# Marking the operations that empty matmul banks as first to be scheduled

## The chip, the cores and the metric

The kernel runs on one core of a Trainium2 chip. The core has a matrix unit (TensorE, "PE" in the profile; its weight loads are "PEld"), VectorE ("DVE"), ScalarE ("ACT"), GpSimd ("POOL") and SyncE ("SP"), whose queue issues most of the DMAs. Each engine works through its own list of instructions in order; between engines they wait on semaphores. The time is that of one execution on the device, in microseconds; the median of several runs is compared.

## The reference

One layer of a streaming encoder, applied to a prompt of 2048 tokens and, with carried state, to 8 samples of 16 tokens. The width is 1024, everything is fp32.

```python
def trunk_layer(x, pos, C0, n0, m0, k_cache, v_cache, conv_prev, mchunk, ...):
    qm, km, vm, om, ip, fp, qa, ka, va = split_in(x @ w_in)      # 4*512 | 8 | 512 | 2*128
    ...
    hm, C1, n1, m1 = mlstm_chunkwise(qm, km, vm, logi, logf, C0, n0, m0, mchunk)
    og = jax.nn.sigmoid(om.astype(jnp.float32)).reshape(B, T, M_HEADS, M_HEAD_DIM)
    hm = (og * head_norm(hm, g_mlstm_norm)).reshape(B, T, M_WIDTH).astype(x.dtype)
    qa = rope(qa.reshape(B, T, A_Q_HEADS, A_HEAD_DIM), pos)
    ka = rope(ka.reshape(B, T, A_KV_HEADS, A_HEAD_DIM), pos)
    ...                                                          # ha: sliding-window attention
    mix = jnp.concatenate([hm, ha], axis=-1) @ w_out
    h = layer_norm(DEEPNORM_ALPHA * x + mix, ln1_g, ln1_b)
    f, conv_rows = conv_ffn(h, conv_prev, w_up, w_conv, b_conv, w_down)
    y = layer_norm(DEEPNORM_ALPHA * h + f, ln2_g, ln2_b)
    return y, (C1, n1, m1, k_rows, v_rows, conv_rows)

def conv_ffn(h, conv_prev, w_up, w_conv, b_conv, w_down):
    u = h @ w_up                                                 # 1024 -> 2 * 2816
    ext = jnp.concatenate([conv_prev.astype(u.dtype), u], axis=1)
    c = b_conv + sum(ext[:, j:j + T] * w_conv[j] for j in range(CONV_W))
    a, g = jnp.split(c, 2, axis=-1)
    return (jax.nn.silu(g) * a) @ w_down, ext[:, -(CONV_W - 1):]
```

Four large projections hold nearly all of the arithmetic: the in-projection (w_in), the output projection (w_out), the up-projection (w_up) and the down-projection (w_down). The mLSTM (a matrix memory with gates), the attention over a window of 128 tokens, the norms, the width-3 convolution and the gate lie between them.

## The kernel before

**How a product is made.** PE multiplies numbers of reduced precision, so each fp32 operand is split into a high part (a cast on ACT, L217) and a low part (a subtraction on DVE, L218; for tokens L564 and L565), and each product is three matmuls: high by high, high by low, low by high. Most projections are cut into blocks of 2 by 2, and these are multiplied in the form that needs seven block products and not eight, numbered by s in the code. The sums of weight blocks and of token blocks that this form needs are made on DVE or read back from DRAM.

**Banks.** Products accumulate in matmul banks (512 fp32 values for each of 128 partitions). The in-projection has three, A, B and C. Products 1 and 2 go to A; 6, 5 and 3 to B; 7 and 4 to C. A bank's sum is carried on from one product to the next where the form allows it; after product 1 ACT copies A to B. Everything that leaves a bank is a copy by ACT or a sum by DVE, and a product that wants the bank anew waits until this operation is done. The order of the products is such that a bank is often read just after the product that fills it and wanted again soon after.

**The stages.** The in-projection (`i_dense`, to about 650 us) runs over token blocks b, column blocks g and the products s. After each product `i_after` empties the bank: copies (L769), the sum `add` (L775), and for g = 2 also the rotary embedding of four DVE operations (`rope`, L866 to L869), for g = 3 the gate's tanh, then the stores to DRAM by the SP queue (`i_store`, L751 for one of them). The mLSTM and the attention of earlier token blocks are woven in between the products by `Chains`: their matmuls stand between those of the projection in PE's list, and their other operations (for instance the mLSTM's output at L1164 to L1179, the attention's softmax at L1319 to L1344, that of the samples at L1502 to L1517) run on the same DVE, ACT and POOL. The output projection (`o_block`, about 650 to 925 us, five token blocks) has plain products; its banks are emptied by one DVE operation each, L1610, which adds the bank to the residual. The first four blocks are normed as they come; the last block's norm (`o_late`, loads L1634, sums L1638 and L1639) runs inside the next stage. The up-projection (`f_ups`, about 915 to 1860 us) runs over 3 token blocks, 22 column pairs j and seven products s, on two sets of three banks. `f_after` copies or adds each bank into the half-rows `u` (L1851 to L1870), and after products 3 and 4 it goes on with the convolution (L1882, L1884), the gate and the store. `f_next` makes the weights of a product 6 products ahead in the first token block, 8 in the others. The down-projection (`f_downs`, to the end) uses eight banks; `S.copy` (L2046) and `add` (L2063 to L2068) empty them into the rows `yacc`, which are normed and stored.

**What sets the order.** PE's list is written by hand: it is the order in which the program states its matmuls (`manual_schedule`, in `run`). The lists of DVE, ACT and POOL and the SP queue are made by the scheduler of the tile framework. It takes operations as they become ready by its own reckoning, and where several are ready it goes by priority, which is the order in which the program states them. Inside `with tc.high_priority():` operations get a priority ahead of all that isn't so marked. Before the change no copy or sum of the projections is marked. In `run`'s in-projection loop, `with self.tc.issue_after(behind)` holds weight loads behind the first copy of a column block.

Of the kernel before, what the change touches and what calls it, by code (L numbers as in the profile page):

```python
# [11 lines left out]
ALU = mybir.AluOpType  # L12
# [16 lines left out]
ALPHA = 2.0 ** 0.25  # L29
# [175 lines left out]
class Prog:  # L205
# [380 lines left out]
    def i_dense(self):  # L586
        nc, a = self.nc, self.a
        nb = len(IBLOCKS)
        last = NG - 1

        self.next_raw()
        self.x_load(0, 2)
        for _ in range(3):
            self.next_raw()
        self.x_load(0, 4)
        self.single_raw = self.tp.tile([P, KD, P], F32, name="xsr", tag="pth", bufs=2)
        nc.sync.dma_start(self.single_raw, a["xs"])
        self.angles = {}
        self.rope_load(IBLOCKS[0][2], 2)
        self.rope_load(NPT, 1)  # L600
        self.next_split()
        self.x_steps(0, "b12")
        for _ in range(3):
            self.next_split()
        self.x_steps(0, 3)
        self.x_single(1, 2)
        self.x_load(0, 1)
        self.next_raw()
        self.x_load(0, 3)
        self.x_steps(0, 1)  # L610
        self.advance()
        self.x_steps(0, 2, "t3", 7, "t2", 6)
        self.x_single(4)
        self.x_steps(0, "t1", 5, "t4")
        self.sb, self.trans = {}, None

        passages = [{1: ["load"], 7: ["t3", 7], 6: ["t2", 6], 3: [3, "t4"], 4: ["b12", "t1"]},
                    {1: ["load"], 6: ["t3"], 7: [7, "t2"], 5: [6], 3: [3, "t4"], 4: ["b12", "t1"]}]
        sums = 0
        after = None  # L620
        for item in self.items:
            if after:

                after[0] -= 1
                if after[0] == 3:
                    self.logs_of(after[1] - 1)
                if after[0] < 0:
                    self.i_done = after[1]
                    after = None
            self.chains.hold = item[0] == "t" and item[1] > 0  # L630
            if item[0] == "t":
                _, b, ti, e = item
                if ("g", e, 3) not in self.wu:
                    self.advance()
                if b not in self.gates:
                    self.gates[b] = self.tp.tile([P, 5, 8], F32, name="gates", tag="gates", bufs=2)
                ps = self.bank([P, 512], "pg") if ti == 4 else self.ib[ti % 2 * 2]
                yield from self.i_direct(b, ti, e, ps)
                self.i_keys(b, ti, ps)
                if ti == 1:  # L640
                    if b + 1 < nb:
                        self.x_steps(b + 1, 1, 2)
                    else:
                        self.release(4)
                    after = [6, b + 1]
                elif ti == 3 and b or ti == 4:
                    self.release(4)
                    self.x_steps(b, 4)
                    if b:
                        self.x_steps(b, 5)  # L650
                self.advance()
                continue
            _, b, g, s = item
            if item not in self.wu:
                self.advance()
            yield from self.i_product(b, g, s)
            del self.wu[item]
            self.release(2)
            if self.trans and s != 4:
                self.i_transposes()  # L660
            behind = self.i_after(b, g, s)
            if (b, g, s) == (0, 0, 7):
                self.t_setup()
            if (g, s) == (1, 6):
                self.rope_load(IBLOCKS[b][0], 2)
            if g == last and b + 1 < nb:
                if s == 7:
                    self.rope_load(IBLOCKS[b + 1][2], 2)
                for x in passages[b > 0].get(s, ()):
                    if x == "load":  # L670
                        self.spare = True
                        self.x_load(b + 1, 1, 2, 3, 4)
                    else:
                        self.x_steps(b + 1, x)
            if g == last and b + 1 == nb and s in (7, 5, 2, 3):
                self.x_pair(0, (7, 5, 2, 3).index(s))
            with self.tc.issue_after(behind) if behind and b == 0 else nullcontext():
                self.advance()

            if b >= nb // 2 and g < last:  # L680

                steps = (6, 2, 5) if g == last - 1 else (6, 5, 3)
                if s in steps:
                    self.d_sums(sums, steps.index(s))
                    sums += s == steps[2]
        self.sums = sums
        self.logs_of(nb - 1)
        self.chains.hold = False
# [897 lines left out]
    def o_block(self, b):  # L1586
        nc, nb = self.nc, len(OBLOCKS)
        tiles = OBLOCKS[b]

        ys = self.ynext + [self.o_x(t) for t in tiles[len(self.ynext):]]  # L1590
        self.ynext = []

        outs = [self.fp.tile([P, D], F32, name="ymix", tag="hst", bufs=2) for _ in tiles] if b == nb - 1 else ys
        for hf in range(2):
            c = slice(hf * 512, hf * 512 + 512)
            steps = 0
            for cost, ti, ps in self.group(b, tiles, 8 * b + 4 * hf, hf == 1):
                yield cost
                if ps is None:
                    steps += 1  # L1600
                    if hf and b + 1 < nb and steps == 8 * len(tiles) - 6:
                        self.ynext = [self.o_x(t) for t in OBLOCKS[b + 1][:2]]
                    if steps % 2 == 0 and self.norms and next(self.norms[0], self) is self:
                        del self.norms[0]
                    if hf == 0 and b and self.sums < NK2 and steps in (2, 14, 20):
                        self.d_sums(self.sums, (2, 14, 20).index(steps))
                        self.sums += steps == 20
                    continue
                y = outs[ti]
                nc.vector.scalar_tensor_tensor(y[:, c], ys[ti][:, c], ALPHA, ps, op0=ALU.mult, op1=ALU.add)  # L1610
                if hf and b < nb - 1:
                    self.norms.append(self.norm(y, *self.ln1, self.zh[tiles[ti]]))
        assert b < nb - 1 or self.sums == NK2
        self.late = list(zip(outs, tiles))
# [164 lines left out]
    def f_ups(self, n):  # L1779
# [11 lines left out]
        for i, (b, j, s) in enumerate(self.seq):  # L1791
# [4 lines left out]
            self.f_product(b, j, s)  # L1796
            while self.made < min(i + 1 + (AHEAD if b == 0 else AHEAD + 2), len(self.seq)):
                self.f_next()
            self.f_after(b, j, s)
            if i < 4:  # L1800
                self.f_tokens(0, *((5,), (3,), ("t4",), (4,))[i])
# [31 lines left out]
            for i, (l, r) in enumerate(((wh, hh), (wh, hl), (wl, hh))):  # L1833
                mm(ps, l[:, k], r[:, k], start=s in (1, 7) and k == 0 and i == 0, stop=k == 3 and i == 2, skip_group_check=True)  # L1834

    def f_after(self, b, j, s):

        nc, f2 = self.nc, self.f2
        V, S = nc.vector, nc.scalar
# [6 lines left out]
        dec = lambda z: z[:, m:].rearrange("p (b l) -> p b l", b=DB)  # L1846
        sam = lambda u: u[:, 2 + WP:2 + n].rearrange("p (b l) -> p b l", b=DB)
        m = WP - h
        half = lambda v: f2.tile([P, 770], F32, name=f"u{v}", tag=f"u{v}", bufs=1)
        if s == 1:  # L1850
            S.copy(B, A)  # L1851
        elif s == 6:
            self.u2[j % 2] = u2 = f2.tile([P, 384], F32, name="ua", tag="ua", bufs=2)[:, :h]
            S.copy(u2, B)
        elif s == 2:
            self.uv = half(0)
            S.copy(self.uv[:, 2:2 + h], A)
        elif s == 5:
            self.ug = u = half(1)
            u4 = f2.tile([P, 384], F32, name="ub", tag="ub", bufs=1)[:, :h]  # L1860
            S.copy(u4, B)
            V.tensor_add(u[:, 2 + h:2 + WP], C[:, :m], u4[:, :m])
            if has_s:
                V.tensor_add(sam(u)[:, :, 2:], dec(C), dec(u4))  # L1864
        elif s == 3:
            S.copy(self.uv[:, 2 + h:2 + WP], B[:, :m])
            if has_s:
                S.copy(sam(self.uv)[:, :, 2:], dec(B))
        elif s == 4:
            V.tensor_add(self.ug[:, 2:2 + h], C, self.u2[j % 2])  # L1870
        if s not in (3, 4):
            return

        v, u = (0, self.uv) if s == 3 else (1, self.ug)
        if v == 0:
# [130 lines left out]
    def f_downs(self):  # L2006
# [35 lines left out]
        def after(s, p):  # L2042
            ps = banks[role[s][2 if p == np_ else p]]
            ta, tb = (tiles[2 * np_], None) if p == np_ else (tiles[p], tiles[np_ + p])
            if s == 1:
                S.copy(banks[role[6][2 if p == np_ else p]], ps)  # L2046
            elif s == 2:
                add(ta, 0, ps, True)
                if ta == last_tile:
# [12 lines left out]

        def add(t, half, ps, first):  # L2063
            y = ys[t][:, half * 512:half * 512 + 512]
            if first:
                V.scalar_tensor_tensor(y, y, ALPHA, ps, op0=ALU.mult, op1=ALU.add)
            else:
                V.tensor_add(y, y, ps)  # L2068

        def finish(t, b, step):  # L2070
            if b == nb - 1 and step == 3:
# [68 lines left out]
```

## Time and profile before

| | |
|---|---|
| time, median of 3 runs | 2336.47 us (2332.86 to 2341.85) |
| profiled execution, its own time | 2337.74 us |
| its span | 2336.0 us |
| mean granted clock of PE | 0.992 |
| PE busy | 2300.5 us (98%) |
| DVE busy | 1818.7 us (78%) |
| ACT busy | 1275.2 us (55%) |
| POOL busy | 253.0 us (11%) |
| DMA | 629.24 MB, mean 269 GB/s |

The profile is that of one execution; the time runs from start to end on the device, the span from the first to the last instruction. Busy times count the work of an engine, not its waiting. The shares are averages over four stages: DVE, at 78% of the whole, is close to full in some stretches of tens of microseconds and has room in others. Rows name an operation by its engine, its line in the kernel and what it writes and reads (`zev<-dps,zev`: tile zev from a bank of the pool dps and zev). A wait is put down to the operation that came last.

### The profile page before, as it was taken

What the parts mean: (1) busy time and instruction counts of PE and PEld (TensorE: products, weight loads), DVE (VectorE), ACT (ScalarE), POOL (GpSimd) and SP (SyncE); (2) the same over time, 40 slices, a digit from 0 to 9 for tenths busy, and PEclk for the clock granted to TensorE, in tenths of its full rate; (3) what the DMA queues carried; (4) which work ended last, traced back from release to release, by engine and by line L of the source; (5) the groups of instructions that cost most, each with busy time, mean ns of one, the idle gap of its engine ahead of it and who ended that gap; (6) DMA issues with size and microseconds to landing.
All of it is one profiled execution on the core that took longest, in us unless ns stands there. A gap on an engine that the chain in (4) does not pass through costs nothing. (4 is left out here: it accounts for less than half of the span.)

```text
span 2336.0 us, 39880 instructions
## 1 busy us (share of the span) xinstructions
PE 2300.5 (98%) x14301; PEld 2112.0 (90%) x14301; DVE 1818.7 (78%) x3187; ACT 1275.2 (55%) x2409; POOL 253.0 (11%) x477
## 2 busy tenths in 40 slices
PE   8999999999999999999999999999999999999998
PEld 8999989998987777999999999999999978888876
DVE  7786587797688888988788776778766786896987
ACT  5453457776766664556556555556554544444452
POOL 0001000000011111211102010102111200100100
PEclk9999999999999999999999999999999999999999
DMA  7888889989987766788777889878998786756753
GB/s 271 293 304 294 285 271 337 318 291 330 327 274 251 233 214 250 268 319 295 265 275 267 311 310 318 304 266 279 308 299 262 224 288 197 258 175 226 251 157 108
DMA packets 298727, 629.24 MB, mean 269 GB/s; under 512 B 47709, under 2 KB 140961, under 8 KB 298529
## 3 DMA queue, kind: packets, MB, share of 16 engines
q1 hardware_dynamic: 294144, 612.99, 76.7%
q0 software_dynamic: 3520, 10.56, 1.4%
q10 hardware_dynamic: 864, 3.15, 0.3%
q8 instruction: 113, 1.85, 0.3%
q14 instruction: 86, 0.70, 0.1%
HBM read 456.01 MB, written 170.59 MB: 268 GB/s over the span
## 5 line engine op out<-in xcount | busy, mean ns | idle before, releaser
L1834 PE MATMUL fup<-hh,uw 128*128 128x384 f32 (+1 forms) x1848 | 480.7, 329 | 2.5 <-DVE uw L218 2.1
L1834 PE MATMUL dps<-hh,uw 128*128 128x384 f32 (+1 forms) x1848 | 478.7, 328 | 3.4 <-DVE u L1864 2.4
L1834 PEld LDWEIGHTS fup<-hh,uw 128*128 128x128 f32 x1848 | 331.6, 189 | 3.7 <-DVE uw L218 2.4
L1834 PEld LDWEIGHTS dps<-hh,uw 128*128 128x128 f32 x1848 | 330.2, 188 | 4.2 <-DVE u L1864 2.7
L1884 DVE SCALAR_TENSOR_TENSOR cc<-u,cw,cc 128x768 f32<-128x768 f32 (+1 forms) x264 | 258.4, 979 | 63.8 <-ACT cc L1882 57.6
L1834 PE MATMUL fup<-hl,uw 128*128 128x384 f32 (+1 forms) x924 | 303.7, 329 | 2.6 <-DVE hl L218 2.5
L1834 PE MATMUL dps<-hl,uw 128*128 128x384 f32 (+1 forms) x924 | 302.5, 327 | 0.0
L702 PE MATMUL dps<-w,oh 128*128 128x256 f32 x1344 | 257.2, 286 | 1.3 <-DVE zev L775 0.8
L217 ACT CAST uw<-wraw 128x1024 fp32r<-128x1024 f32 x126 | 123.0, 979 | 225.5 <-PE dps L2039 119.9
L218 DVE TENSOR_TENSOR w<-wraw,w 128x1024 fp32r<-128x1024 f32 (+2 forms) x167 | 189.0, 1139 | 55.4 <-ACT w L217 54.3
L217 ACT CAST w<-wraw 128x1024 fp32r<-128x1024 f32 (+2 forms) x167 | 162.9, 983 | 119.1 <-PE dps L702 57.1
L702 PEld LDWEIGHTS dps<-w,oh 128*128 128x128 f32 x1344 | 212.5, 189 | 12.8 <-issue 8.9
L218 DVE TENSOR_TENSOR uw<-wraw,uw 128x1024 fp32r<-128x1024 f32 x126 | 142.3, 1131 | 66.2 <-ACT uw L217 66.0
L702 PE MATMUL dps<-w,ol 128*128 128x256 f32 x672 | 188.8, 281 | 0.0
L1834 PEld LDWEIGHTS fup<-hl,uw 128*128 128x128 f32 x924 | 174.5, 189 | 3.3 <-DVE hl L218 3.2
L2039 PE MATMUL fup<-uw,fu 128*128 128x512 f32 x726 | 174.5, 396 | 1.7 <-DVE uw L218 1.7
L702 PE MATMUL dps<-oh,w 128*128 128x256 f32 x896 | 170.7, 285 | 5.3 <-ACT zev L769 3.2
L1834 PEld LDWEIGHTS dps<-hl,uw 128*128 128x128 f32 x924 | 173.6, 188 | 0.0
L2039 PEld LDWEIGHTS fup<-uw,fu 128*128 128x128 f32 x726 | 136.8, 189 | 35.2 <-DVE uw L218 2.1
L2039 PE MATMUL dps<-uw,fu 128*128 128x512 f32 x660 | 165.2, 395 | 1.1 <-DVE uw L218 1.1
L1882 ACT ACTIVATE cc<-u,cw 128x768 f32<-128x768 f32 (+1 forms) x132 | 132.2, 1002 | 56.4 <-DVE u L1870 30.0
L702 PEld LDWEIGHTS dps<-oh,w 128*128 128x128 f32 x896 | 142.0, 191 | 11.9 <-issue 4.1
(323 smaller groups left out, 4594.7 us busy)
## 6 DMA issues: line engine op xcount, KB each, us to landing
uw<-zw SPq DMA_DIRECT2D x176, 512.0 KB, 5.3
zw<-uw SPq DMA_DIRECT2D x88, 512.0 KB, 2.9
w<-zws SPq DMA_DIRECT2D x72, 512.0 KB, 6.4
wv<-wup SPq DMA_DIRECT2D x66, 512.0 KB, 4.5
wraw<-wi SPq DMA_DIRECT2D x65, 512.0 KB, 5.1
wraw<-zt SPq DMA_DIRECT2D x60, 512.0 KB, 4.2
wraw<-wdn SPq DMA_DIRECT2D x45, 512.0 KB, 4.1
wraw<-wo SPq DMA_DIRECT2D x40, 512.0 KB, 4.8
```

Of the source, the lines that this page charges most:

```text
L217: nc.scalar.copy(hi, src)
L218: nc.vector.tensor_sub(lo, src, hi.bitcast(F32))
L702: mm(o, l, r, start=s in (1, 7) and c == k == i == 0, stop=k == 3 and i == 2, skip_group_check=True)
L1834: mm(ps, l[:, k], r[:, k], start=s in (1, 7) and k == 0 and i == 0, stop=k == 3 and i == 2, skip_group_check=True)
L1882: S.activation(c[:, v], u[:, 2:2 + n], AF.Identity, bias=w[3], scale=w[2])
L1884: V.scalar_tensor_tensor(c[:, v], u[:, i:i + n], w[i], c[:, v], op0=ALU.mult, op1=ALU.add)
L2039: mm(ps, l[:, k, c], r[:, k], start=s in (1, 4, 7) and u == 0 and k == 0 and i == 0, stop=u == nu - 1 and k == n - 1 and i == 2, skip_grou ...
```

## The change

Four places that empty banks are put under `tc.high_priority()`: the whole of `i_after` in the in-projection, with its rotary operations, tanh and stores; the sum of the output projection; the copies and sums of the up-projection, which are cut out of `f_after` into a function of their own, `f_evict`; and the copy and the sums of the down-projection. No operation is added, removed or resized, and the program states them in the same order.

```diff
             if self.trans and s != 4:
                 self.i_transposes()
-            behind = self.i_after(b, g, s)
+            with self.tc.high_priority():
+                behind = self.i_after(b, g, s)
...
                 y = outs[ti]
-                nc.vector.scalar_tensor_tensor(y[:, c], ys[ti][:, c], ALPHA, ps, op0=ALU.mult, op1=ALU.add)
+                with self.tc.high_priority():
+                    nc.vector.scalar_tensor_tensor(y[:, c], ys[ti][:, c], ALPHA, ps, op0=ALU.mult, op1=ALU.add)
...
                 self.f_next()
+            with self.tc.high_priority():
+                self.f_evict(b, j, s)
             self.f_after(b, j, s)
...
-    def f_after(self, b, j, s):
+    def f_evict(self, b, j, s):
...
         elif s == 4:
             V.tensor_add(self.ug[:, 2:2 + h], C, self.u2[j % 2])
+
+    def f_after(self, b, j, s):
+
         if s not in (3, 4):
             return
+        nc = self.nc
+        V, S = nc.vector, nc.scalar
+        n, WP, has_s, sam = self.fshape
...
             if s == 1:
-                S.copy(banks[role[6][2 if p == np_ else p]], ps)
+                with self.tc.high_priority():
+                    S.copy(banks[role[6][2 if p == np_ else p]], ps)
...
-            if first:
-                V.scalar_tensor_tensor(y, y, ALPHA, ps, op0=ALU.mult, op1=ALU.add)
-            else:
-                V.tensor_add(y, y, ps)
+            with self.tc.high_priority():
+                if first:
+                    V.scalar_tensor_tensor(y, y, ALPHA, ps, op0=ALU.mult, op1=ALU.add)
+                else:
+                    V.tensor_add(y, y, ps)
```

More of the change, by code (lines that the diff above doesn't have):

```diff
@@ L1848, in f_after @@
         m = WP - h
+        self.fshape = n, WP, has_s, sam
         half = lambda v: f2.tile([P, 770], F32, name=f"u{v}", tag=f"u{v}", bufs=1)
```

## The prediction

> **What bounds the kernel now.** I read the page first, then what the matrix unit (PE) waited for, then the timeline and windows around each of these waits.
>
> ```profile
> span 2336.0 us, 39880 instructions
> ...
> PE 2300.5 (98%) x14301; PEld 2112.0 (90%) x14301; DVE 1818.7 (78%) x3187; ACT 1275.2 (55%) x2409; POOL 253.0 (11%) x477
> ```
>
> PE is the bound: it stands for 2336.0 − 2300.5 = 35.5 us in all. The change orders only the other engines, so it can take away a part of these 35.5 us, or add to them. The waits of PE on operations that empty a bank (engine and line waited for; total us, times, longest):
>
> ```profile
> PE dps L728 <- DVE zev L775: 3.7, 2, 2.2
> PE dps L702 <- ACT zev L769: 3.2, 2, 2.5
> ...
> PE dps L1834 <- DVE u L1864: 2.4, 1, 2.4
> ...
> PE dps L1834 <- DVE u L1862: 0.6, 1, 0.6
> ```
>
> These are 3.7 + 3.2 + 2.4 + 0.6 = 9.9 us in six places: 0.4% of the time. A stall can also lower the clock behind it. In the view of windows (stretch in us; its length; busy us and count of PE, weight loads, DVE, ACT, POOL; granted clock; DMA share; GB/s):
>
> ```profile
> 306.45:310.20 3.75, 3.75 (x18) 3.75 (x19) 3.75 (x4) 1.05 (x1) 0.00 (x0) 0.54 0.61 188
> 310.20:313.95 3.75, 3.75 (x33) 3.75 (x33) 3.75 (x8) 2.33 (x4) 0.00 (x0) 1.00 0.80 217
> 472.86:476.30 3.44, 3.44 (x28) 3.44 (x29) 3.37 (x4) 2.73 (x6) 0.00 (x0) 1.00 0.65 220
> ...
> 1000.00:1600.00 600.00, 599.28 (x3481) 597.96 (x3480) 466.41 (x595) 337.32 (x545) 79.49 (x162) 1.00 0.81 290
> 924.60:928.00 3.40, 3.40 (x12) 3.40 (x11) 3.40 (x6) 0.46 (x1) 0.00 (x0) 0.50 0.70 282
> 900.00:938.00 38.00, 33.02 (x154) 28.24 (x153) 37.68 (x44) 23.09 (x32) 5.93 (x4) 0.91 0.59 214
> ```
>
> After the stall that ends at 306.45 PE does 18 matmuls in 3.75 us at a clock of 0.54; in the next 3.75 us it does 33. The spell costs (33 − 18) × 3.75/33 = 1.7 us. After the stall that ends at 472.86 the clock stays 1.00. The first stall is 2.23 us long, the second 1.51 (rows below), and a third, of 2.10, ends at 923.25 and has its spell too (0.50 from 924.60): a stall from somewhere between 1.51 and 2.10 us on costs 1.7 us more than itself. The fourth window says that 600 us of the up-projection hold 600 − 599.28 = 0.72 us without PE: nothing to win there.
>
> By the Trainium skill (TensorE: Matmul & The Clock Gate, "Why this matters for your kernels") only idle gaps above about 3 us drop the clock. The trace differs: 0.54 behind 2.23 us. By that rule no stall here would touch the clock and both clock terms below would go; they cancel (−1.7 and +1.7), so the sum would be the same.
>
> **The change part by part.** No operation is added or removed, and PE's order, written by hand, is the same. In the built programs 784 of DVE's 3187 operations change their place, most by one or two; ACT keeps 1983 of 2278 in place. DVE and ACT work in order, so an operation put earlier delays what it passes, and one put in front of a bank that isn't full yet makes its engine stand.
>
> Gains. The rows (start, us, engine, line, out<-in, shapes, and in brackets the idle time before and what ended it):
>
> ```profile
> 304.58 1.22 DVE L565 TENSOR_TENSOR ol<-xr,oh 128x1024 fp32r<-128x1024 f32 x1
> 305.72 0.68 DVE L775 TENSOR_TENSOR zev<-dps,zev 128x512 f32<-128x512 f32 x1
> 306.45 0.39 PE L728 MATMUL dps<-w,oh 128*128 128x264 f32 x1 [2.23 <-DVE zev L775]
> ...
> 334.27 0.58 PE L702 MATMUL dps<-oh,w 128*128 128x256 f32 x1 [2.49 <-ACT zev L769]
> ...
> 472.12 0.68 DVE L775 TENSOR_TENSOR zev<-dps,zev 128x512 f32<-128x512 f32 x1
> ...
> 472.86 0.39 PE L728 MATMUL dps<-w,oh 128*128 128x264 f32 x1 [1.51 <-DVE zev L775]
> ...
> 923.25 0.44 PE L1834 MATMUL fup<-hh,uw 128*128 128x384 f32 x1 [2.10 <-DVE uw L218]
> ...
> 932.12 1.74 DVE L218 TENSOR_TENSOR hl<-hraw,hh 128x1536 fp32r<-128x1536 f32 x1
> ...
> 933.92 0.44 PE L1834 MATMUL fup<-hl,uw 128*128 128x384 f32 x1 [2.49 <-DVE hl L218]
> ...
> 1857.63 0.55 DVE L218 TENSOR_TENSOR fu<-r,fu 128x384 fp32r<-128x384 f32 x1
> ...
> 1858.70 0.42 PE L1834 MATMUL dps<-hh,uw 128*128 128x320 f32 x1 [2.44 <-DVE u L1864]
> ```
>
> At 306 the sum of L775 now stands ahead of the token split L565: it starts at 304.58 instead of 305.72, −1.14. The stall left is 1.09 us, below 1.51, so the slow spell goes as well, −1.7. At 472 the product before had ended at 472.86 − 1.51 = 471.35; the sum now stands ahead of two operations and can start at 471.4 instead of 472.12: −0.7, with no clock to win. At 334 the copy of L769 keeps its place on ACT: 0; likewise the other ACT wait. At 1588 (the wait of 0.6 on L1862) the sum passes what held it: −0.6. At 1858 both sums pass the split fu (0.55): −0.5; 1.9 us stay, between 1.51 and 2.10, so that the spell there may or may not go (0 to −1.7; I take 0, as 1.9 is nearer to the 2.10 of the next place, which has its spell). Between 900 and 938 the stalls are on splits, and DVE is busy 37.68 of 38 us: reordering shifts them. There the split hl (932.12) comes only one weight split earlier: −0.6 (0 to −1.5). Sum: −1.14 − 1.7 − 0.7 − 0.6 − 0.5 − 0.6 = −5.2, with ends of −3 and −8.
>
> Losses. What is passed on DVE is, in three places, the head of a chain that PE waits for:
>
> ```profile
> 251.13 0.16 DVE L1505 TENSOR_SCALAR amx<-amx 128x4 f32<-128x4 f32 x1
> ...
> 253.50 0.69 DVE L869 TENSOR_TENSOR zev<-zev,rb 128x512 f32<-128x512 f32 x1
> ...
> 252.33 0.40 ACT L1507 ACTIVATE scs<-scs,amx 128x144 f32<-128x144 f32 x1
> ...
> 255.82 0.33 PE L1516 MATMUL ppt<-ident,scs 128*128 128x128 f32 x1 [0.22 <-POOL scs L1510]
> ...
> 414.11 1.28 ACT L1166 ACTIVATE hn<-hn,ms 128x128 f32<-128x128 f32 x4
> ...
> 417.27 1.22 DVE L218 TENSOR_TENSOR w<-wraw,w 128x1024 fp32r<-128x1024 f32 x1
> ...
> 419.33 0.60 PE L1176 MATMUL pht<-ident,hn 128*128 128x128 f32 x4
> ...
> 697.57 1.20 DVE L218 TENSOR_TENSOR w<-wraw,w 128x1024 fp32r<-128x1024 f32 x1
> 697.75 1.71 ACT L1321 ACTIVATE sc<-sc,asm 128x256 f32<-128x256 f32 x4 [1.35 <-DVE asm L1319]
> 698.50 1.35 PE L1343 MATMUL ppt<-ident,sc 128*128 128x128 f32 x8
> ...
> 699.95 0.68 DVE L1610 SCALAR_TENSOR_TENSOR ymix<-ymix,dps 128x512 f32<-128x512 f32 x1
> ```
>
> At 251 the sum and the whole rotary chain of a column block (to L869, which ends at 254.2) with a weight split now stand ahead of the sample attention's L1505. That moves from 251.13 to about 254.1, its exponential on ACT from 252.33 to 254.2, and PE's transpose, which already waited 0.22, from 255.82 by +1.9. The stall is then 2.1, as long as the 2.10 of 923, so the slow spell comes: +1.7 (0 to 1.7). At 414 the same chain and the split of 417.27 pass the scale of the mLSTM's output (L1164); its four activations start about 419.2 instead of 414.11, the first done at 419.6, the last at 420.5, while PE wants them from 419.33 on: +1.0 (0 to 1.3). In the output projection at 698 two sums of L1610 (2 × 0.68, of which 0.42 falls into DVE's own idle time) and the split of 697.57 (1.20) pass the reciprocal that releases ACT's L1321. It moves by 1.36 − 0.42 + 1.20 = 2.1; ACT's first piece had been done at 697.75 + 1.71/4 = 698.2, 0.3 ahead of PE: +1.8 (0 to 2.1, and 1.7 more if the clock drops). Four smaller places of that kind (about 60, 833, 1259 and 1666 us) I put at 0.4 each, +1.6; an estimate, from one passing sum of 0.68 and half of it hidden (0 to 1 each). Sum: 1.9 + 1.7 + 1.0 + 1.8 + 1.6 = +8.0, with ends of 0 and +12.
>
> Moved DMAs: the stores of a finished block (in i_after) follow its sums in the SP queue, ahead of some loads; a store waits for the sum, and what is behind it waits along. The up-projection's sums and the down-projection's copies and sums change places with splits that PE needs only products later (PE stands for 0.72 us in 600): 0, as long as that cover holds; without it a passing sum costs its 0.68.
>
> Net: 8.0 − 5.2 = +2.8. On the profiled execution's 2337.74 us that is 2340.5; that execution lies 1.27 above the median of the runs, 2336.47, so 2339.2 is comparable; I say 2339.0.
>
> **The rivals.** *It wins what the waits show.* All six waits on emptied banks vanish (−9.9), and with them the slow spells at 306, 334 and 1858 (3 × 1.7): −15.0, so 2336.47 − 15.0 = 2321.5. For it: the waits are real and name exactly the marked operations. Against: the ACT copy of 334 isn't moved at all, and at 306 and 472 the stall left is the sum's own run after the product's end.
>
> By the clock rule of the skill cited above this rival would end at 2336.47 − 9.9 = 2326.6, within half a per cent.
>
> *It does nothing.* The scheduler already took most marked operations as they came ready, PE's order is fixed, and what is passed has slack: 2336.5. For it: a quarter of DVE's operations move, but mostly by one or two places. Against: the stall of 306 has a plain cause that the new order removes.
>
> *The late norm's load stands in DVE's way* (slower). The norm of the last output block runs inside the up-projection; its second half's sums (L1638) need gains loaded by L1634:
>
> ```profile
> 975.58 0.69 DVE L218 TENSOR_TENSOR uw<-uw 128x512 fp32r<-128x512 f32 x1
> ...
> 988.95 0.42 SPq L1634 DMA_DIRECT2D lnp<-ln_g  x1
> ...
> 995.84 0.75 DVE L1638 SCALAR_TENSOR_TENSOR ymix<-ymix,lmv,lnp 128x512 f32<-128x512 f32 x1
> ...
> DMA to landing us min/median/max: 4.8/5.1/5.4
> ...
> 960.00:1010.00 50.00, 50.00 (x289) 50.00 (x289) 46.81 (x72) 28.95 (x51) 13.66 (x16) 1.00 0.84 308
> ```
>
> In the changed order these sums stand right behind the split of 975.58. If the load still lands at 988.95 + 5.4 = 994.3, DVE stands 18 us with all weight splits behind it; it has 50 − 46.81 = 3.2 us to spare there, so PE loses 14.8 and a slow spell of 1.7: 2336.47 + 16.5 = 2353. Against: the load's issue moves up in the SP queue too, and with 4.8 to 5.4 us to landing it is then there before DVE asks. It decides, over half a per cent, from a landing after about 989.5.
>
> **How the numbers follow.** Half a per cent (11.7 us) is about what a measurement of this kernel can tell from no change. Chances: the small net loss 0.55; no effect 0.26; the full gain 0.06, as three of its places are contradicted by the orders; the late load 0.13, as it needs the SP queue to hold back a load that the new order puts ahead. The first two lie within half a per cent: faster 0.06, same 0.81, slower 0.13. Range: the gains at their largest with no loss give 2336.47 − 8 = 2328.5; the losses at their largest with the smallest gains 2336.47 + 12 − 3 = 2345.5, and the spell at 698 and part of the late load's case bring it to 2349. Left out is the full gain and the late load, 0.19.
>
> **What would show it.** Right: the waits of PE on L775 at 306 and 472 fall to about 1.1 and 0.8, with no slow spell at 306; new waits of PE of 1 to 2 us on POOL L1510 near 256, on ACT L1166 near 419 and on ACT L1321 near 698, one with a spell; the ACT wait of 334 stands as it was; PE is gapless between 1000 and 1600. Wrong: waits on weight splits behind 976, DVE idle before L1638, or SP-queue stores that hold back weight loads so that PE waits on DMA.

## The result

The changed kernel takes 2340.32 us (median of 22 runs, 2337.10 to 2345.99); the kernel before, run beside it, 2336.34 us (22 runs, 2327.41 to 2343.61). The ratio is 1.0022, with a 95% interval of 1.0013 to 1.0031. By the ratio that is +5.1 us (3.0 to 7.2); the two medians alone lie 4.0 us apart. The change is slower by less than half a per cent. The time lies inside the forecast range and close to its 2339.0; the difference is larger than the +2.8 us that was forecast.

The page of the changed kernel:

```profile
span 2335.3 us, 39857 instructions
...
PE 2298.1 (98%) x14301; PEld 2108.5 (90%) x14301; DVE 1819.9 (78%) x3187; ACT 1273.2 (55%) x2409; POOL 259.7 (11%) x477
```

Its profiled execution, at 2337.10 us, happens to be the fastest of the 22, so the span says nothing of the loss. The waits do. Line numbers in the changed kernel are 1 higher than before from the in-projection on, 2 behind the output projection's sum, and more from there (L1834 is now L1838). What PE waited for (engine and line; total us, times, longest):

```profile
PE dps L703 <- ACT zev L770: 4.5, 2, 3.9
PE fup L1838 <- DVE hl L218: 4.3, 2, 3.7
PE ppt L1517 <- POOL scs L1511: 2.3, 1, 2.3
...
PE dps L1838 <- DVE u L1869: 2.0, 1, 2.0
...
PE ppt L1344 <- ACT sc L1322: 1.5, 1, 1.5
...
PE pht L1177 <- ACT hn L1167: 0.8, 1, 0.8
```

The waits for sums of the in-projection (two rows on L775 before, of 3.7 and 0.8 us; the line is now L776) are gone from the list. Three others have come or grown: on POOL L1511 (0.2 us before), on ACT L1322 and on ACT L1167 (none and 0.3, the latter at another place). They belong to the softmax of the samples, the softmax in the output projection and the mLSTM's output. The wait for ACT's copy has grown from 3.2 to 4.5. Summed over all its matmuls, PE's idle time ahead of them is 27.9 us before and 29.7 us now.

How the new ones come about, on the timeline of the changed kernel around 251 us (start, us, engine, line, out<-in, idle time before and what ended it):

```profile
250.53 0.68 DVE L870 TENSOR_TENSOR zev<-zev,rb 128x512 f32<-128x512 f32 x1
251.13 0.16 DVE L1503 SCALAR_TENSOR_TENSOR amx<-amx,k_sinkx 128x4 f32<-128x4 f32 x1
251.21 1.22 DVE L218 TENSOR_TENSOR w<-wraw,w 128x1024 fp32r<-128x1024 f32 x1
...
252.53 0.17 DVE L1506 TENSOR_SCALAR amx<-amx 128x4 f32<-128x4 f32 x1
...
252.79 0.42 ACT L1508 ACTIVATE scs<-scs,amx 128x144 f32<-128x144 f32 x1
...
256.25 0.33 PE L1517 MATMUL ppt<-ident,scs 128*128 128x128 f32 x1 [2.29 <-POOL scs L1511]
```

The last three rotary operations (only L870 is shown) and a weight split of 1.22 us now come ahead of L1506, a step of 0.17 us on which ACT's exponentials, POOL's scaling and PE's transpose hang one after the other. At 698 us:

```profile
693.07 1.39 DVE L1612 SCALAR_TENSOR_TENSOR ymix<-ymix,dps 128x512 f32<-128x512 f32 x2
...
696.87 1.22 DVE L218 TENSOR_TENSOR w<-wraw,w 128x1024 fp32r<-128x1024 f32 x1
...
698.10 0.14 DVE L1320 RECIPROCAL asm<-asm 128x4 f32<-128x4 f32 x1
...
698.33 1.71 ACT L1322 ACTIVATE sc<-sc,asm 128x256 f32<-128x256 f32 x4 [2.47 <-DVE asm L1320]
698.89 0.33 PE L1344 MATMUL ppt<-ident,sc 128*128 128x128 f32 x1 [1.47 <-ACT sc L1322]
```

Two sums of the output projection and a split stand ahead of a reciprocal of 0.14 us; ACT stands 2.47 us for it and PE 1.47.

**A measure that a single span isn't.** PE's list is the same in all kernels here, so the n-th matmul of one trace can be set against the n-th of another. The stretches below begin and end with the matmuls that start at 60, 650, 915 and 1860 us in the trace of before. The times are those of one execution each, so kernels whose marks in a stretch agree serve as repeats of one another. The columns hold the traces of this and the next sections, but for the two kernels that move work to GpSimd; in the in-projection, kernels that mark only a part of `i_after` stand apart.

| stretch | without marks in it | with the change's marks in it |
|---|---|---|
| in-projection from 60 us | 590.3, 587.7, 590.9, 586.9, 588.5: mean 588.9 | 591.4, 589.2, 594.6: mean 591.7 |
| output projection | 264.8, 264.5, 264.6, 264.5, 264.6, 266.8: mean 265.0 | 268.6, 268.4, 267.9, 268.7: mean 268.4 |
| up-projection, 915 to 1860 | 945.0, 946.1, 945.4, 945.8, 945.0, 944.7: mean 945.3 | 943.2, 942.4, 942.5, 942.7, 941.5: mean 942.5 |

So the loss is +2.8 in the in-projection and +3.4 in the output projection, and the up-projection gives 2.9 back: +3.3 in all, within the interval of the times. PE's stands are only a part of this: of the +2.8 in the in-projection, 0.8 is more idle time of PE, 1.1 is lost to more half clock (means of the same traces), and 1.0 is neither. The in-projection differs by 4 to 5 us between executions of the same order; what that is, the second set of experiments shows.

### The profile page after: what moved, and what is told of

It reads as the page before. It is cut to its first block, busy times and chain, and to the rows that moved or that the text cites. A ratio compares the mean times of both kernels' runs of the same rounds, so it can differ in the third digit from the quotient of the medians.

```text
span 2335.3 us, 39857 instructions
## 1 busy us (share of the span) xinstructions
PE 2298.1 (98%) x14301; PEld 2108.5 (90%) x14301; DVE 1819.9 (78%) x3187; ACT 1273.2 (55%) x2409; POOL 259.7 (11%) x477
## 5 line engine op out<-in xcount | busy, mean ns | idle before, releaser
L1838 PE MATMUL fup<-hh,uw 128*128 128x384 f32 (+1 forms) x1848 | 480.1, 329 | 1.6 <-ACT fup L1856 1.0
L1838 PE MATMUL dps<-hh,uw 128*128 128x384 f32 (+1 forms) x1848 | 478.2, 328 | 2.3 <-DVE u L1869 2.0
L1838 PEld LDWEIGHTS fup<-hh,uw 128*128 128x128 f32 x1848 | 331.5, 189 | 2.4 <-ACT fup L1856 1.3
L1838 PEld LDWEIGHTS dps<-hh,uw 128*128 128x128 f32 x1848 | 330.0, 188 | 2.8 <-DVE u L1869 2.2
L1838 PE MATMUL fup<-hl,uw 128*128 128x384 f32 (+1 forms) x924 | 303.8, 329 | 4.3 <-DVE hl L218 4.3
L1838 PE MATMUL dps<-hl,uw 128*128 128x384 f32 (+1 forms) x924 | 302.6, 327 | 0.0
L1838 PEld LDWEIGHTS fup<-hl,uw 128*128 128x128 f32 x924 | 174.4, 189 | 5.1 <-DVE hl L218 4.9
L1838 PEld LDWEIGHTS dps<-hl,uw 128*128 128x128 f32 x924 | 173.6, 188 | 0.0
```

## The experiments

### One part of the change at a time

Each kernel keeps the marks of one stage and takes off the others.

```diff
 e1_in: only this
+            with self.tc.high_priority():
+                behind = self.i_after(b, g, s)
 e2_out: only this
+                with self.tc.high_priority():
+                    nc.vector.scalar_tensor_tensor(y[:, c], ys[ti][:, c], ALPHA, ps, op0=ALU.mult, op1=ALU.add)
 e3_up: only this
+            with self.tc.high_priority():
+                self.f_evict(b, j, s)
 e4_down: only S.copy in after() and the sums in add()
```

> Only the in-projection's marks (the whole of i_after). By the sum of places: in the stretch from 60 to 650 us of the kernel before, PE stands 0.6 us longer in the changed kernel's trace (8.9 against 8.3): 2.1 more at 256, 1.4 at 334, 0.8 at 419, 0.6 at 531, and less by 2.2 at 306, 1.5 at 472, 0.8 at 584. With a half-clock spell won at 306 and one lost at 256 the time should be 2336.3 + 0.6 = 2337 (2335 to 2339.5), the output projection's stretch (264.8 us) unchanged. Rival, the marks act together: with one part alone the schedule behind it settles differently and the loss of the whole change (4 us) or none of it shows here.

> Only the output projection's mark. By the sum of places: the stand of 1.5 us on ACT's scaling near 698 and the half-clock spell behind it, worth 1.7, come with it: the output projection's stretch goes from 264.8 to 268.5 us, the rest of the trace as before; 2336.3 + 3.3 = 2339.6 (2338 to 2341.5). That would be most of the change's loss. Rival, the spell is chance: the stand is there without a spell, +1.6. Rival, the marks act together: no stand at 698 without the in-projection's marks, 2336.3.

> Only the up-projection's marks. By the sum of places: from 915 us on PE stands as long as before within 0.3 us (2.1 less at 923, 1.0 and 1.2 more at 928 and 934; 0.6 more at 1259 and 1641 each, 1.0 less at 1588 and 1686, 0.5 less at 1859), and a spell behind 1859 may go: 2336.3 - 0.5 = 2335.8 (2334 to 2338). Rival, the late norm's load holds DVE up: not in the changed kernel's trace, so no more than 2338 here either.

> Only the down-projection's marks. Two sums change their place by one: no change, 2336.3 (2335 to 2338), and the stands of PE from 1860 us on are 2.9 us as before. Rival: a loss here that the trace of the changed kernel hides in a spell, 2338 or more.

Measured against before, with intervals:

| | median us | ratio | 95% interval |
|---|---|---|---|
| e1_in | 2339.54 | 1.0019 | 1.0010 to 1.0028 |
| e2_out | 2336.68 | 1.0011 | 1.0000 to 1.0022 |
| e3_up | 2333.95 | 0.9999 | 0.9990 to 1.0007 |
| e4_down | 2334.41 | 0.9999 | 0.9991 to 1.0008 |
| before, beside them | 2334.80 | | |

The parts add up: 0.19 + 0.11 − 0.01 − 0.01 = 0.28% against 0.22% for the whole. The in-projection's marks carry most of the loss; with +4.4 us (2.3 to 6.5) that is more than the +0.6 expected, and what the rival said, that the whole loss shows there. The output projection's cost +2.6 (0 to 5.1) without a half-clock spell behind 698 in this trace: stand yes, spell no, as its rival had it. Yet its stretch takes 267.9 us, near the 268.5 that was forecast with a spell, so the spell isn't what makes it long. The up- and down-projection's marks make no difference that the times can show. The interval of e3_up, −2.3 to +1.6 us, doesn't hold the 2.9 us that the up-projection's stretch gains in the traces, so that gain isn't confirmed.

What e1_in's expectation had wrong is 306. I had counted the stand there as cured, from 2.2 us to 0 in the changed kernel's trace. Without that gain the sum of stands is +2.8 and not +0.6, and +4.5 with the half-clock spell at 256; both lie in the measured interval. In e1_in, with the same order, the stand is back:

```profile
308.71 0.69 DVE L1107 TENSOR_TENSOR dt<-k_mcau,wi 128x512 f32<-128x512 f32 x1 [4.25 <-DMA wi<-zM]
309.32 0.68 DVE L776 TENSOR_TENSOR zev<-dps,zev 128x512 f32<-128x512 f32 x1
...
310.06 0.69 PE L729 MATMUL dps<-w,oh 128*128 128x264 f32 x2 [2.34 <-DVE zev L776]
```

The sum is where the change puts it, right behind L1107 and ahead of the token split. But VectorE has stood 4.25 us for a load, and the sum with it. The trace of before has the same wait, a row ahead of those that the prediction shows, and in the changed kernel's own trace the load was simply there:

```profile
303.97 0.69 DVE L1106 TENSOR_TENSOR dt<-k_mcau,wi 128x512 f32<-128x512 f32 x1 [3.00 <-DMA wi<-zM]
```

```profile
301.85 0.69 DVE L1107 TENSOR_TENSOR dt<-k_mcau,wi 128x512 f32<-128x512 f32 x1 [0.28 <-DMA wi<-zM]
302.46 0.68 DVE L776 TENSOR_TENSOR zev<-dps,zev 128x512 f32<-128x512 f32 x1
```

And in e2_out and e4_down, whose orders in the in-projection are those of before, PE does not stand at 306 at all, while it does in e3_up, which has that order too. Over the traces of both orders, with VectorE's wait for the load against PE's stand:

| | before | e3_up | e8_but | e4_down | e2_out | e1_in | changed | e11_again |
|---|---|---|---|---|---|---|---|---|
| sum ahead of the split | no | no | no | no | no | yes | yes | yes |
| VectorE waits for wi<-zM, us | 3.0 | 3.4 | 1.2 | 0.5 | 0 | 4.2 | 0.3 | 0.6 |
| PE stands at 306, us | 2.2 | 2.6 | 0.4 | 0 | 0 | 2.3 | 0 | 0 |

In these eight traces the stand goes with the load and not with the order.

### What rides along, where the 306 comes from, and which sums cost in the output projection

e5_ops marks, in the in-projection alone, only the operation that reads a bank:

```diff
+        with nullcontext() if i else self.tc.high_priority():
+            if g == 3:
+                nc.scalar.activation(ev, src, AF.Tanh, scale=0.5)
+            elif not i:
+                nc.scalar.copy(ev, src)
...
+        first = self.tc.high_priority
...
+        def copy(d, x):
+            with first():
+                return nc.scalar.activation(d, x, AF.Copy, scale=KSCALE) if g < 2 else nc.scalar.copy(d, x)
...
+            with first():
+                if g < 2:
+                    V.scalar_tensor_tensor(u, C, KSCALE, u, op0=ALU.mult, op1=ALU.add)
+                else:
+                    V.tensor_add(u, C, u)
```

> Only in the in-projection, and there only the one operation that reads a bank is marked (copy, sum, scaled copy, tanh); the rotary operations, the gate's +1 and the stores behind it are not. Theory, the loss comes from what rides along with the sums: the stands at 256 (2.3 us, with its half-clock spell of 1.7) and at 419 (0.8) go, those at 472 (1.0 to 1.7) and 584 (0.8) stay away: 4.8 us less than with all of i_after marked, and about 2 us less than before, 2334.8 - 2 = 2333 (2331 to 2335.5). Rival, the sum itself (0.69 us) in front of the softmax's small operations is enough: the stand at 256 stays above 1.5 us and the time above 2337.

Measured: 2331.19 us against 2335.82, ratio 0.9978 (0.9968 to 0.9988): 5.1 us faster than before, and the in-projection takes 585.2 us. In its trace the chain's step (here L1513) is ahead of the third rotary operation and of the split, and of the stand 0.67 us are left:

```profile
250.29 0.42 DVE L875 TENSOR_TENSOR rb<-zev,ropet 128x256 f32<-128x256 f32 x1
250.63 0.16 DVE L1513 TENSOR_SCALAR amx<-amx 128x4 f32<-128x4 f32 x1
250.74 0.69 DVE L876 TENSOR_TENSOR zev<-zev,ropet 128x512 f32<-128x512 f32 x1
251.35 1.22 DVE L218 TENSOR_TENSOR w<-wraw,w 128x1024 fp32r<-128x1024 f32 x1
...
255.21 0.33 PE L1524 MATMUL ppt<-ident,scs 128*128 128x128 f32 x1 [0.67 <-POOL scs L1518]
```

At 419, 472 and 584 PE doesn't stand at all. So what costs is not the sum put first but what was marked with it; the loss turned into a gain, larger than the 2 us expected. Which of the followers costs isn't separated: the rotary operations, the +1 and the stores lose their marks together, and with them the samples' block (`i_batch`, which `i_after` calls), its copies out of a bank included. Part of the surplus is that in this order the mask's subtraction at the load wi<-zM stands behind other work of VectorE, where it waits for nothing, and the stand at 306 is zero:

```profile
310.84 0.68 DVE L1114 TENSOR_TENSOR dt<-k_mcau,wi 128x512 f32<-128x512 f32 x1
```

e6_pool has no marks. The subtraction of the first mLSTM tile alone goes to GpSimd:

```diff
-            self.nc.vector.tensor_sub(dt, mask, pm)
+            (self.nc.gpsimd if self.first_tile else self.nc.vector).tensor_tensor(dt, mask, pm, op=ALU.subtract)
...
+        self.first_tile = t == 0
```

> The kernel before, without any mark; the mask's subtraction (L1106) of the first mLSTM tile is done by GpSimd, so that VectorE no longer stands for the load wi<-zM at its head. Theory, the stand of PE at 306 comes from this load: in six traces PE stands 2.2, 2.6 and 2.3 us there where VectorE had stood 3.0, 3.4 and 4.2 us for the load, and not at all where it stood 0.5 us or less. Then PE does not stand at 306 here, whatever the run: 2334.8 less half of (2.3 + 1.7), so 2332.8 (2331 to 2335). Rival, the order of split and sum makes it, as the prediction said: a stand of 1.1 us or more stays at 306.

Measured: 2342.09 us against 2335.82, ratio 1.0030 (1.0019 to 1.0042). The stand at 306 is gone, as the load's theory says, and the time is a miss: the wait went on to the next engine.

```profile
303.95 1.27 POOL L1106 TENSOR_TENSOR dt<-k_mcau,wi 128x512 f32<-128x512 f32 x1 [5.22 <-DMA wi<-zM]
...
305.26 0.70 ACT L1119 ACTIVATE wi<-wi 128x128 f32<-128x128 f32 x2 [4.07 <-POOL dt L1106]
...
302.36 0.68 DVE L775 TENSOR_TENSOR zev<-dps,zev 128x512 f32<-128x512 f32 x1
```

The sum runs at 302.36, unhindered. GpSimd stands 5.22 us for the load, ScalarE 4.07 us for GpSimd, and behind it in ScalarE's list are casts and copies that PE needs. From the list of PE's waits:

```profile
PE dps L702 <- ACT dps L797: 4.2, 1, 4.2
...
PE dps L728 <- ACT gates L737: 1.5, 1, 1.5
```

The second stands at 311, the first at 381; whether the first hangs on the load too, or on the other places that the scheduler changed between 306 and 400 us, isn't settled.

e7_mix joins e5_ops, the up-projection's marks and this move to GpSimd.

> The bank readers of the in-projection alone, the up-projection's marks, and the subtraction of the first mLSTM tile on GpSimd; no mark in the output and the down-projection. If the parts add up: -2 from the first, -2 from the last, and from the up-projection's marks the 2.4 us by which the stretch from 960 to 1860 was shorter in the two traces that have them: 2334.8 - 6.4 = 2328.5 (2326 to 2332), faster than both kernels. Rival, the gains are given back at 334, where PE waits for a copy that ScalarE reaches late: its stand grows from 2.5 to about 4, and the time is 2331 to 2334.

Measured: 2334.75 us, ratio 1.0000 (0.9987 to 1.0014): no gain, and above the rival's range too. Its in-projection takes 593.3 us against 585.2 without the move, with stands of 1.8 us at 311, 1.3 at 368, 1.9 at 381 and 3.7 at 334. The rival's place, 334, is only one of them.

e8_but marks the output projection's sums but for the three of the first block's second half, the two at 693 us among them:

```diff
-                with self.tc.high_priority():
+                with nullcontext() if b == 0 and hf else self.tc.high_priority():
```

> The output projection's mark alone, left off for the second half of the first token block, whose two sums stand at 693 us ahead of the softmax's reciprocal. Theory: the stand of 1.5 us near 698 goes, and the stretch from 650 to 915 us takes 265 to 266 us and not 268; the time is 2334.8 + 0.7 = 2335.5 (2334 to 2337). Rival, it is the sum of many small delays over five blocks: the stretch stays above 267, the time at 2336.7 or more.

Measured: 2334.96 us, ratio 1.0006 (0.9994 to 1.0018); the output projection takes 265.7 us, and PE doesn't stand at 698. Of the 3.4 us that the mark costs there, 2.7 go when it comes off the three sums of the first block's second half, two of which are those at 693. That is read from the stretches; the intervals of the two times, this one and e2_out's, overlap.

### A better mix, and the change with one thing taken back

e9_both is e5_ops with the up-projection's marks. e10_ride is the changed kernel in which the in-projection marks only the bank readers, as in e5_ops. e11_again is the changed kernel as it is.

> The bank readers of the in-projection alone and the up-projection's marks; no mark in the output and the down-projection, nothing moved to GpSimd. If the parts add up: 4.6 us below before from the first (measured), and up to 2.4 from the second (the stands at 1588 and 1686 go, the one at 1859 is 0.5 shorter, that at 1259 0.5 longer): 2335.8 - 7 = 2329 (2327 to 2331.5). Rival, the up-projection's marks bring nothing, as their run alone (0.9999) allows: 2331.2 or more.

> The changed kernel with one thing taken back: in the in-projection only the operation that reads a bank is marked, not the rotary operations, the +1 and the stores. Theory: its loss of 4 to 5 us turns into a gain; before, less 4.6 for the in-projection, plus 2.6 for the output projection's marks, less 0 to 2 for the up-projection's: 2335.8 - 3 = 2333 (2330.5 to 2335). Rival, the marks behind the in-projection weigh more than their runs alone said: 2337 or more.

> The changed kernel as it is, for a second trace of it. The stands at 256 (2.3 us), 419 (0.8) and 698 (1.5) are there again, within 0.2 us, and none at 472 and 584. At 306 PE stands for 2.3 us if VectorE's wait for the load wi<-zM is over 3 us, and not at all if it is below 0.5. The half-clock spell behind 256 comes again; those behind 698 and 1859 may not. Rival: the stand at 256 is as much a matter of the run as that at 306.

| | median us | before, beside it | ratio | 95% interval |
|---|---|---|---|---|
| e9_both | 2329.52 | 2334.76 | 0.9980 | 0.9968 to 0.9992 |
| e10_ride | 2331.79 | 2334.76 | 0.9990 | 0.9980 to 1.0001 |
| e11_again | 2337.98 | 2334.76 | 1.0017 | 1.0003 to 1.0030 |

e9_both is faster than both kernels, by 4.7 us (1.9 to 7.5) against before; whether it beats e5_ops isn't settled, as 0.9978 and 0.9980 don't differ. e10_ride shows the same cause from the other side: with the rotary operations, the +1 and the stores unmarked, and all else as changed, 1.0022 becomes 0.9990. Its in-projection takes 584.7 us, its output projection still 268.7.

e11_again has the stands of the changed kernel again, at 256, 419 and 698 to within 0.02 us. They belong to the order. Its wait for the load is 0.6 us and it doesn't stand at 306. But behind the stand at 256, which is 2.27 us here and was 2.29 in the first trace, the clock differs, against the expectation. The windows behind that stand (length; busy us and count of PE, weight loads, DVE, ACT, POOL; granted clock; DMA share; GB/s), first of the changed kernel, then of e11_again:

```profile
257.20:260.60 3.40, 3.40 (x19) 3.40 (x18) 0.00 (x0) 1.89 (x3) 0.00 (x0) 0.50 0.81 288
```

```profile
255.90:259.30 3.40, 3.40 (x30) 3.15 (x28) 0.83 (x1) 2.60 (x4) 0.00 (x0) 1.00 0.87 276
```

The same stand costs 1.7 us more in one execution than in the other.

What differs is where it falls on a grid of time. In each of the 13 traces the half-clock spells begin at whole multiples of 3.413 us from one another, to within 0.002 us. The first line below is the stretch of this grid just ahead of the changed kernel's spell; the other two are those over which the stand of e11_again spreads:

```profile
253.79:257.20 3.41, 1.12 (x11) 0.87 (x10) 0.34 (x2) 0.71 (x4) 1.15 (x1) 1.00 0.94 286
```

```profile
250.98:254.39 3.41, 1.72 (x15) 1.51 (x13) 0.74 (x5) 1.91 (x9) 0.62 (x1) 1.00 0.90 290
254.39:257.80 3.41, 2.83 (x25) 2.76 (x26) 0.00 (x0) 1.46 (x3) 0.52 (x1) 1.00 0.87 295
```

PE was busy for 1.12 us of 3.41 in the one, for 1.72 and 2.83 in the others. From 60 to 2310 us, over all 13 traces, each of the 42 full-clock stretches of the grid in which PE was busy for less than 1.5 us is followed by a spell. Of the stretches with more, only 16 are: two that hold mostly transposes, near 698, and 14 in which PE doesn't stand at all but runs the samples' attention, 21 or more products of 64 columns (L1525 and L1526 of the kernel before). With 19 or fewer of these no spell follows, with 21 one did not. One of these, in e4_down, and the spell behind it:

```profile
286.20:289.60 3.40, 3.40 (x28) 2.59 (x28) 1.40 (x3) 1.97 (x4) 0.00 (x0) 1.00 0.99 271
289.60:293.00 3.40, 3.40 (x19) 3.25 (x18) 3.26 (x7) 0.00 (x0) 0.00 (x0) 0.50 0.76 237
```

This is read from the traces; no kernel here was made to move a stand along the grid.

## Why the prediction was right, and where its steps were not

The forecast was +2.8 us, by a sum of small stands, and the measured difference is +5.1 (3.0 to 7.2), so the forecast lies just under the interval. The direction and the mechanism hold: PE's list is untouched, VectorE works in order, the marked operations come earlier, and the chains that they pass come later. By its steps:

- *256 us, +1.9.* Right: the stand went from 0.2 to 2.3 us in all three traces of that order. Named right down to the engines, L1506, ACT, POOL, PE. The spell of +1.7 came in two of the three, but it is not a net cost: between 250 and 300 us the clock is at half for 6.8, 6.8 and 3.4 us in these three traces, and for 6.8, 6.8, 6.8, 3.4 and 3.4 in the five of the order before, which have no stand above 0.3 us there.
- *419 us, +1.0.* Right: 0.8 in all three. The loss is larger than the stand. The four transposes behind it take 1.21 us and not 0.60, as each waits for its piece of ScalarE's work, and the stretch from 410 to 420 us is 1.6 longer in each of the three:

```profile
418.89 1.21 PE L1177 MATMUL pht<-ident,hn 128*128 128x128 f32 x4 [0.81 <-ACT hn L1167]
```

- *698 us, +1.8.* Right in place, cause and nearly in size: 1.5 in all four traces with the mark. A spell followed in two of the four.
- *306 us, −1.14 and −1.7.* The step that failed. The order changed as said, but the stand comes from a wait of VectorE for a load, which the prediction didn't look at: the idle time in front of L1106, one row ahead of the rows that it quoted. With the load late the stand is there in the changed order too (2.3 us), with the load early it isn't there before either. None of the 2.8 us can be put down to the change.
- *472 us, −0.7, and 584, left out.* Too small: the stands are 1.5, 1.7, 1.0, 1.3 and 1.5 in the five traces of the order before and zero in the three with the marks, and the 0.8 at 584 goes as well. Together about −2.2. The prediction's sum of 9.9 us passed over the row of 0.8 at 584, and two of 0.4 and 0.3 on ScalarE's copies in the up-projection (L1851, L1861).
- *334 us, 0.* The copy kept its place, as said. But PE reaches it earlier where it has lost less before, and stands longer: 3.9, 3.9 and 2.9 against 2.5 to 3.3 in the order before. ScalarE is late there by its own work, so a gain ahead of it is partly given back.
- *900 to 938 us, −0.6.* A shift, as the view of windows said: the stands between 923 and 934 sum to 4.6 before and 4.7 in the changed kernel, in other places. The places change between executions of one order too: e4_down, with the order of before, has 1.0, 0.5 and 3.3.
- *Output projection outside 698, +0.4.* Too small: the whole stretch takes 3.4 us more. The idle time of PE there is 2.2 to 3.1 us in the four traces with the mark, against 0.5 to 0.6 in five of the six without it (1.9 in e5_ops), and a spell of 1.7 stands in two of the four; the rest is spread, and without a cause shown.
- *Up-projection, −0.6 and −0.5, and +0.4 each at 1259 and 1666.* Right in kind: the stand at 1588 goes, that at 1859 falls from 2.4 to 2.0, that at 1259 grows from 0.1 to 0.6 and one of 0.6 appears at 1641, none at 1666. The stretch gains 2.9 in the traces and not 0.3, more than the stands explain; the times of e3_up don't confirm it, and it stays open.
- *The clock.* The prediction read from two stalls that lengths from between 1.51 and 2.10 us on bring a spell. That fell: 2.27 us at 256 brought none in one execution and 2.29 did in another; 1.47 us at 698 brought one in the changed kernel and none in e11_again; and there are spells, at 288 for instance, that follow no stand. By the grid above it is how long PE runs within one stretch of 3.41 us that counts. The terms −1.7 and +1.7 were each a chance and not a price.

The rivals: the full gain is out, since 334 stayed and 306 wasn't the order's. No effect is out as well, with an interval that begins at 1.0013. The late norm's load didn't hold VectorE up: it landed in 3.4 to 4.6 us, and the sums ran without a wait:

```profile
975.54 1.28 DVE L218 TENSOR_TENSOR uw<-uw 128x512 fp32r<-128x512 f32 x2
976.74 1.40 DVE L1640 SCALAR_TENSOR_TENSOR ymix<-ymix,lmv,lnp 128x512 f32<-128x512 f32 x2
```

That the sum came out as near as it did is in part luck, as its errors went both ways: 2.8 us of gain at 306 weren't the change's and the output projection lost 1.2 more than counted, while 472 and 584 gave 1.5 more and the up-projection, in the traces, 2.6 more.

## What to carry to other kernels

Mark the one operation that frees the bank and not the block around it: the same places with the followers unmarked went from 1.0019 to 0.9978. Before a stall is put down to the order of two operations, look at what their engine was waiting for ahead of both; and before a stall is counted as a gain, look for it in a second execution of the same order, since those at 256, 419 and 698 came every time and the one at 306 at full length in three of eight. Ahead of moving work up, ask which short operations at the head of a chain across three engines are passed: 0.17 and 0.14 us of VectorE's work held PE for 2.3 and 1.5 us.

## What the runs showed of the hardware that I had not expected

- The half-clock spells are not set by the length of a stall alone (2.27 us without, 1.47 us with, and some without any). They last 3.41 us or twice that, and which stalls they follow changes between executions of one program. They lie on a grid of 3.413 us that sits differently in each execution: a stand of 2.3 us brings one where most of it falls into one stretch of the grid (PE busy 1.12 of 3.41 us), and none where it is split over two (1.72 and 2.83). The Trainium skill (TensorE: Matmul & The Clock Gate, "What's actually happening") describes a window of about 3.4 us that runs free of the program, which agrees with the lengths seen here; its rule on idle gaps above about 3 us ("Why this matters for your kernels") doesn't cover the spells behind 1.5 to 2.5 us.
- One load's landing decides 2.3 us: wi<-zM, issued by GpSimd, makes VectorE wait 0 to 3.4 us in the five traces of the order before and 0.3 to 4.2 us in the three of the changed one. In the in-projection, executions of one order differ by 4 us (586.9 to 590.9), and the two slowest of the five are the two that stand at 306. These two also lose 1.7 us more to the half clock between 250 and 300 us than e2_out and e4_down.
